# Gate rows for the last expert's result: from a DRAM scratch by transfers instead of from transposes

## The chip, the cores and the metric

The kernel runs on one core of one Trainium2 chip. The metric is device time in microseconds. Of the engines, PE is TensorE (matmuls; PEld its weight loads), DVE is VectorE, ACT is ScalarE, POOL is GpSimd and SP is SyncE, which here only issues transfers. Each engine works through its own instructions in the order of the program. Transfers issued by SP and by ACT are carried out by the same 16 DMA engines.

## The reference, cut to what matters

One layer runs over two streams of 128 tokens with 1024 channels each. A mixer comes first, then a mixture of 32 experts of which each token uses four, then a final norm:

```
x = x + g2 * moe(h)          # g2: one gate value per stream (2) and channel (1024)
moe(h) = sum over e of w_tok[e] * (act_e(h @ w_gu[e] + b_gu[e]) @ w_down[e] + b_down[e])
y = rmsnorm(x) * norm_final
```

The change concerns `g2` where it multiplies the result of the last expert. The values themselves are part of the adaLN modulation and are known long before the experts begin.

## The kernel before

The mixer fills about the first 475 us. After it the experts are worked through one by one, e = 0 to 31, some 27 us each. An expert's weights are six units of 2 MB: units 0 to 3 are quarters of `w_gu`, units 4 and 5 halves of `w_down`. They stream from HBM through eleven places in SBUF; `w31_3` below is unit 3 of expert 31, and where a place is split in two, the halves are called a and b. SP issues each load when PE has read the unit that held its place.

An expert runs so: PE multiplies the gathered tokens by `w_gu` (`e30pgu`, L1229, with the bias at L1235); DVE clamps the one half (`e30gm`, L1255), ACT takes the tanh (`e30tg`, L1256), DVE makes the product (`e30gm`, L1261 and L1262); PE transposes it (`e30pat`, L1299), ACT copies it out (`e30aT`, L1302), and PE multiplies by `w_down` (`e30py`, L1312). Results are added to the tokens two experts at a time: PE scatters a pair's rows with 0/1 matrices `sT` (`e28pc`, L1327), and DVE multiplies by the gate and adds to `xT` (L1177). The last pair is treated apart. The bias rows and expert 30's result are scattered in two batches (`papc`, L1337), one before expert 31's first product and one behind its last.

For expert 31 the gate is applied ahead of the scatter, since that leaves less behind the last matmul: L1528 multiplies `e31py` by a tile `gslot`, in which a channel's gate stands in a column and is repeated down the rows (64 rows of each half of the channels for each stream). `gates_by_slot` (L1494 to L1505) builds it in the SBUF place `spare`, which held `w30_1`. PE transposes the gate columns of `fin`, spread over 128 columns, into a PSUM bank (`pgs`, L1503: 16 transposes of 128x128), and ACT copies the 64 rows that are wanted into `spare` (L1504: four copies). PE's order in the experts is the order in which the code is written; ACT, DVE, SP and POOL are ordered by a scheduler. `fin` itself is filled on POOL at L1018 once the modulation is known.

Each transfer of SP and ACT counts itself done on one of eight counters, DMAHW0 to DMAHW7, which are handed out in turn in the order of the program. A transfer takes a counter only after the transfer that had it before has landed, and the wait for that stands at the issuing engine, ahead of the issue. So each transfer waits for the one eight places earlier, whichever of the two engines issued that one.

Of the kernel before, what the change touches and what calls it, by code (L numbers as in the profile page):

```python
# [9 lines left out]
F32 = mybir.dt.float32  # L10
# [10 lines left out]
P = 128  # L21
D = 1024
# [5 lines left out]
CAP = 64  # L28
# [35 lines left out]
def hybrid_step(ctx, tc, A):  # L64
    nc = tc.nc
    V, S, G, PE = nc.vector, nc.scalar, nc.gpsimd, nc.tensor
# [14 lines left out]
    phase = weights.enter_context(ExitStack())  # L81
    s1 = phase.enter_context(tc.tile_pool(name="s1", bufs=1))
    ps = ctx.enter_context(tc.tile_pool(name="ps", bufs=1, space=PSUM))
    dr = mixer.enter_context(tc.tile_pool(name="dr", bufs=1, space=bass.MemoryType.DRAM))

    def bank(tag, name, bufs):
        return ps.tile([P, 512], F32, name=name, tag=tag, bufs=bufs)
# [22 lines left out]
    def col(name, j, n=1):  # L110
        return prm[:, COL[name] + j:COL[name] + j + n]
# [29 lines left out]
    ident = con.tile([P, P], F32, name="ident")  # L141
# [796 lines left out]
    for h in range(4):  # L938
        sl, k = slice(4 * h, 4 * h + 4), slice(4 * (h % 2), 4 * (h % 2) + 4)
# [77 lines left out]
    fin = con.tile([P, 3, KC], F32, name="fin")  # L1017
    G.tensor_copy(fin[:, 0:2], mod[:, 40:48, :].rearrange("p k s -> p s k"))  # L1018
    G.tensor_copy(fin[:, 2], col("norm_final", 0, 8))

    lgb = mc.tile([P, 2, NE], F32, name="lgb")
    plr = bank("E", "plr", 1)
# [422 lines left out]
    def expert(e):  # L1445
# [16 lines left out]
        if e > 1:  # L1462
            last = down(e - 1)
            if e % 2:
                scatter_pair(e - 1)
            if e == NE - 1:
                gates_by_slot(spare)

                first = [(ys[e - 1][k // 4][own(0, k // 4), k % 4 * P:(k % 4 + 1) * P], sT[e - 1][own(0, k // 4), k // 4]) for k in range(KC)]
                add_two(bias, first, 0, "C", 2)  # L1470

            load_pieces(6 * e + NUNIT)
# [17 lines left out]
    def own(i, h):  # L1490

        return slice(CAP, P) if i ^ h else slice(0, CAP)
# [3 lines left out]
    def gates_by_slot(spare):  # L1496

        for s in range(2):
            t = spare[:, 512 + 512 * s:1024 + 512 * s]
            for h in range(2):  # L1500
                pt = bank("C", f"pgs{s}{h}", 2)
                for k in range(4):
                    PE.transpose(pt[:, k * P:(k + 1) * P], fin[:, s, 4 * h + k:4 * h + k + 1].to_broadcast([P, P]), ident)  # L1503
                S.copy(t[own(1, h)], pt[own(1, h)])  # L1504
            gslot.append(t)  # L1505

    w = last = mores = None
# [116 lines left out]
def build(nc, ins):  # L1624
    A = {k: nc.dram_tensor(f"in_{k}", v.shape, mybir.dt.from_np(v.dtype), kind="ExternalInput").ap()
         for k, v in ins.items()}
    for k, shape in _OUTS.items():
        A[k] = nc.dram_tensor(k, shape, F32, kind="ExternalOutput").ap()
    with tile.TileContext(nc, schedule_with_timeline_sim=True) as tc:  # L1629
        hybrid_step(tc, A)  # L1630
# [15 lines left out]
```

## Time and profile before

| | us |
|---|---|
| runs (median; lowest to highest) | 1434.77; 1432.7 to 1436.01 |
| profiled execution, its own time | 1434.98 |
| profiled execution, span of the trace | 1433.2 |
| PE busy in the span | 1345.4 (94%) |
| ACT busy in the span | 335.0 (23%) |

The span runs from the first to the last instruction; the 1.8 us around it are the same execution's. A "busy" share is an average over the whole span, in which a mixer bound by PE is followed by experts that also live from the weight stream. What an edit near the end is worth is therefore read from the last 80 us alone.

### The profile page before, as it was taken

How to read it: one execution, taken by the hardware profiler on the slowest of the kernel's cores; microseconds unless marked ns; L12 is line 12 of the kernel's file. 1: busy time of each engine (PE TensorE's matmuls, PEld its weight loads, DVE VectorE, ACT ScalarE, POOL GpSimd, SP SyncE). 2: the span in 40 equal slices, each digit the busy share in tenths (PEclk: the TensorE clock that was granted, in tenths of full speed). 3: DMA queues.
4: the chain of work that ended last, by engine and by line, in shares of the span. 5: the costliest groups of instructions: out<-in, count | busy, mean ns of one | idle time of the engine just before them, and what ended most of it. 6: DMA issues, size and time to landing. Idle time of an engine off the chain costs nothing. (4 is left out here: it accounts for less than half of the span.)

```text
span 1433.2 us, 21073 instructions
## 1 busy us (share of the span) xinstructions
PE 1345.4 (94%) x8637; PEld 798.1 (56%) x8637; DVE 591.3 (41%) x1259; ACT 335.0 (23%) x623; POOL 101.8 (7%) x114
## 2 busy tenths in 40 slices
PE   7999999999999999999999899999999999889897
PEld 3988989898999643443444344344344343343343
DVE  4856879998776322132132222213213212222133
ACT  2534656575664110010000000001000000000011
POOL 1112313431002000000000000000000000000000
PEclk8999999999999999999999999999999999999998
DMA  9997566556877899999999999999999999999981
GB/s 359 294 277 190 201 228 233 214 187 221 314 285 264 331 404 424 425 426 423 423 425 426 412 424 423 424 426 424 423 425 426 423 426 424 426 424 425 424 346 37
DMA packets 84717, 506.52 MB, mean 353 GB/s; under 512 B 6850, under 2 KB 35138, under 8 KB 52418
## 3 DMA queue, kind: packets, MB, share of 16 engines
q1 hardware_dynamic: 81666, 497.71, 87.2%
q10 hardware_dynamic: 2880, 6.60, 1.3%
q8 instruction: 98, 1.61, 0.5%
q14 instruction: 73, 0.60, 0.1%
HBM read 498.26 MB, written 5.64 MB: 352 GB/s over the span
## 5 line engine op out<-in xcount | busy, mean ns | idle before, releaser
L303 DVE TENSOR_TENSOR wl<-win,wh 128x1024 fp32r<-128x1024 f32 (+1 forms) x84 | 101.2, 1216 | 35.7 <-ACT wh L302 23.6
L302 ACT CAST wh<-win 128x1024 fp32r<-128x1024 f32 (+1 forms) x84 | 83.9, 1010 | 72.4 <-PE pbc L330 19.2
L193 POOL TENSOR_TENSOR rf<-rf0v,mhalf 128x1 f32<-128x1 f32 x1 | 0.9, 860 | 948.8 <-DVE rf0v L191 948.8
L714 POOL TENSOR_TENSOR m<-m_half,adt 128x512 fp32r<-128x512 f32 x32 | 43.4, 1374 | 87.1 <-PE pss L717 87.1
L330 PE MATMUL pxs<-hT,wh 128*128 128x256 f32 x256 | 37.5, 291 | 0.0
L330 PE MATMUL pz<-hT,wh 128*128 128x256 f32 x256 | 36.7, 288 | 0.0
L330 PE MATMUL pgt<-hT,wh 128*128 128x256 f32 x256 | 36.0, 287 | 0.3 <-ACT wh L302 0.3
L330 PE MATMUL pbc<-hT,wh 128*128 128x256 f32 x256 | 35.6, 287 | 0.0
L330 PEld LDWEIGHTS pxs<-hT,wh 128*128 128x128 f32 x256 | 32.5, 190 | 3.6 <-issue 2.8
L330 PE MATMUL pso<-yhl,wh 128*128 128x256 f32 x256 | 34.1, 284 | 0.0
L330 PEld LDWEIGHTS pgt<-hT,wh 128*128 128x128 f32 x256 | 32.4, 191 | 2.3 <-issue 1.9
L330 PEld LDWEIGHTS pz<-hT,wh 128*128 128x128 f32 x256 | 32.5, 190 | 1.6 <-issue 1.6
L330 PEld LDWEIGHTS pbc<-hT,wh 128*128 128x128 f32 x256 | 32.2, 190 | 1.9 <-issue 1.7
L330 PEld LDWEIGHTS pso<-yhl,wh 128*128 128x128 f32 x256 | 32.1, 192 | 0.0
L330 PE MATMUL pglu<-hT,wh 128*128 128x256 f32 x192 | 26.8, 290 | 0.0
L330 PEld LDWEIGHTS pglu<-hT,wh 128*128 128x128 f32 x192 | 24.8, 197 | 0.7 <-issue 0.7
L303 DVE TENSOR_TENSOR wl<-wso,wh 128x1024 fp32r<-128x1024 f32 x16 | 19.4, 1218 | 7.5 <-ACT wh L302 7.3
L697 ACT ACTIVATE gd<-gm,dtT 128x128 f32<-128x128 f32 x64 | 20.8, 414 | 4.4 <-DVE gm L688 4.3
L698 DVE SCALAR_TENSOR_TENSOR gd<-gm,dtT,gd 128x128 f32<-128x128 f32 x64 | 20.9, 374 | 1.6 <-ACT gd L697 1.2
L302 ACT CAST wh<-wso 128x1024 fp32r<-128x1024 f32 x16 | 16.7, 1046 | 14.3 <-PE pso L330 10.8
L330 PE MATMUL pwo<-mhl,wh 128*128 128x256 f32 x128 | 18.9, 290 | 0.3 <-DVE mhl L1008 0.3
L1229 PE MATMUL e26pgu<-w,xg 128*64 128x512 f32 x64 | 16.1, 656 | 3.2 <-DMA w<-in_w_gu 2.9
(1098 smaller groups left out, 2639.6 us busy)
## 6 DMA issues: line engine op xcount, KB each, us to landing
w<-in_w_gu SPq DMA_DIRECT2D x116, 2048.0 KB, 31.1
w<-in_w_down SPq DMA_DIRECT2D x57, 2048.0 KB, 27.1
win<-in_w_in_pack SPq DMA_DIRECT2D x38, 1024.0 KB, 5.6
ada<-in_w_ada SPq DMA_DIRECT2D x10, 1024.0 KB, 9.0
wso<-in_w_ssd_out SPq DMA_DIRECT2D x8, 1024.0 KB, 5.8
im<-dru SPq DMA_DIRECT2D x16, 312.0 KB, 8.6
wcf<-in_w_conf_out SPq DMA_DIRECT2D x4, 1024.0 KB, 8.6
wo<-in_w_o SPq DMA_DIRECT2D x4, 1024.0 KB, 9.8
```

What stands on the lines that cost most here:

```text
L193: rstd_ins[0] = G.tensor_tensor(r, v, mhalf[:, 0:n], ALU.pow)
L302: S.copy(hi[:, ks, 0:m], w[:, ks])
L303: V.tensor_tensor(lo[:, ks, 0:m], w[:, ks], hi[:, ks, 0:m], ALU.subtract)
L330: last_wo[0] = PE.matmul(out, w[:, k, 0:n], m[:, k, :], start=first and i == 0, stop=last and i == len(order) - 1, skip_group_check=True)
L697: S.activation(gd[s][:, h, :], gm[:, 0, s, :], AF.Copy, scale=dtT[:, 0, s, c0:c0 + 1])
L698: V.scalar_tensor_tensor(gd[s][:, h, :], gm[:, 1, s, :], dtT[:, 0, s, 32 + c0:33 + c0], gd[s][:, h, :], op0=ALU.mult, op1=ALU.add)
L714: G.tensor_tensor(m4[d], m_half[:, d, None, None, :].to_broadcast([P, 2, 4, 64]), ac[d], ALU.mult)
L1229: PE.matmul(banks[i][m * q:m * q + m, 0:wd], xg[:, k, :], w[k][:, c0:c0 + wd], start=(k == 0), stop=False, skip_group_check=True)
```

## The change

The gate rows are no longer made by PE and ACT late in the kernel. Behind the copy that fills `fin`, ACT now issues two transfers that write the two streams' gates, channel after channel, to a DRAM scratch `grow` of 2 x 1024 values (each value is an element of 4 bytes for itself, since a partition of `fin` holds channels 128 apart). In `gates_by_slot` four transfers on ACT's queue read 512 values each and repeat them over 64 rows of `spare`. The 16 transposes and four copies are gone.

```
+    gdr = ctx.enter_context(tc.tile_pool(name="gdr", bufs=1, space=bass.MemoryType.DRAM))
...
     G.tensor_copy(fin[:, 2], col("norm_final", 0, 8))
+    grow = gdr.tile([2, D], F32, name="grow")
+    for s in range(2):
+        S.dma_start(grow[s].rearrange("(k p) -> p k", p=P), fin[:, s])
...
             for h in range(2):
-                pt = bank("C", f"pgs{s}{h}", 2)
-                for k in range(4):
-                    PE.transpose(pt[:, k * P:(k + 1) * P], fin[:, s, 4 * h + k:4 * h + k + 1].to_broadcast([P, P]), ident)
-                S.copy(t[own(1, h)], pt[own(1, h)])
+                S.dma_start(t[own(1, h)], grow[s:s + 1, 512 * h:512 * h + 512].to_broadcast([CAP, 512]))
```

PE's order around expert 30's end, before and then after, loses one piece and nothing else moves (`pst30` are the scatter matrices of experts 30 and 31, `b_dn` the bias rows):

```order
L1283 MATMUL pst30_22459<-ident_126,sg30_22454 128x128 x4
L1503 MATMUL pgs00_22466<-ident_126,fin_5449 128x128 x4
L1503 MATMUL pgs01_22472<-ident_126,fin_5449 128x128 x4
L1503 MATMUL pgs10_22478<-ident_126,fin_5449 128x128 x4
L1503 MATMUL pgs11_22484<-ident_126,fin_5449 128x128 x4
L1337 MATMUL papc00_22490<-spare_22413,b_dn_22414 128x256
```

```order
L1316 MATMUL e30py_22433<-w30_5_21917,e30aT_22430 64x512 x8
L1287 MATMUL pst30_22464<-ident_128,sg30_22459 128x128 x4
L1341 MATMUL papc00_22475<-spare_22418,b_dn_22419 128x256
L1341 MATMUL papc01_22476<-spare_22418,b_dn_22419 128x256
L1341 MATMUL papc00_22475<-spare_22418,b_dn_22419 128x256
```

The 16 transposes between `pst30` and `papc` are gone.

On ACT the place moves. Before, the four copies stood behind expert 30's other work; the rows name what each waits for:

```order
L1256 ACTIVATE e30tg_22375<-e30gm_22374 128x512 [waits DVE_49,Activation_49]
L1302 COPY e30aT_22430<-e30pat_22429 128x512 [waits DVE_49,PE_49]
L1320 COPY y300_22426<-e30py_22428 64x512 [waits PE_49]
L1286 COPY sT30_22464<-pst30_22459 128x512 [waits PE_49]
L1504 COPY spare_22413<-pgs00_22466 64x512 [waits DMAHW4_49,DMAHW3_49,DMAHW7_49,DMAHW0_49,PE_49]
```

After, on ACT, the four transfers stand ahead of the tanh of expert 30:

```order
L1505 DMA spare_22418<-grow_5454 64x512 [waits DMAHW5_49,DMAHW6_49,DMAHW2_49,DMAHW7_49,DMAHW1_49,PE_49]
L1505 DMA spare_22418<-grow_5454 64x512 [waits DMAHW0_49]
L1505 DMA spare_22418<-grow_5454 64x512 [waits DMAHW1_49]
L1505 DMA spare_22418<-grow_5454 64x512 [waits DMAHW2_49]
L1260 ACTIVATE e30tg_22380<-e30gm_22379 128x512 [waits DVE_49,Activation_49]
L1306 COPY e30aT_22435<-e30pat_22434 128x512 [waits DVE_49,PE_49]
L1324 COPY y300_22431<-e30py_22433 64x512 [waits PE_49]
```

They moved ahead of `e30tg`, and they take counters 7, 0, 1 and 2. Who had these counters last stands in SP's order after the change (each load waits for, and then takes, the counter that it names):

```order
L403 DMA w31_0a_21919<-in_w_gu 128x2048 [waits DMAHW6_49,PE_49]
L403 DMA w31_0b_21921<-in_w_gu 128x2048 [waits DMAHW7_49,PE_49]
L403 DMA w31_1_21923<-in_w_gu 128x4096 [waits DMAHW0_49,PE_49]
L403 DMA w31_2_21925<-in_w_gu 128x4096 [waits DMAHW1_49,PE_49]
L403 DMA w31_3_21927<-in_w_gu 128x4096 [waits DMAHW2_49,PE_49]
L403 DMA w31_4_21929<-in_w_down 128x2048 [waits DMAHW3_49,PE_49]
L403 DMA w31_4_21929<-in_w_down 128x2048 [waits DMAHW4_49]
L403 DMA w31_5_22493<-in_w_down 128x2048 [waits DMAHW5_49,PE_49]
L403 DMA w31_5_22493<-in_w_down 128x2048 [waits DMAHW6_49]
```

Counters 7, 0, 1 and 2 were last taken by `w31_0b`, `w31_1`, `w31_2` and `w31_3`, which stand ahead of the four transfers in the program.

In the mixer the two writes of `grow` stand on ACT here:

```order
L698 ACTIVATE gd71_4091<-gm7_4085,dtT_540 128x128 x2
L1023 DMA grow_5454<-fin_5451 128x8x1 [waits DMAHW1_49,Pool_49]
L1023 DMA grow_5454<-fin_5451 128x8x1 [waits DMAHW2_49]
L303 CAST wh77_4409<-win38_4407 128x1024 [waits PE_49]
L895 ACTIVATE gates_1450<-pgt6_4242,bg_278 128x256 [waits PE_49]
```

They come between `gd71` and the cast `wh77`, which followed each other directly before. `wh77` needs the load that counter 1 stands for, so that it waited for that counter itself.

## Rows read from the trace of the kernel before

**Rows 1.** The page: span, and the share of each slice (40 slices)

```profile
span 1433.2 us, 21073 instructions
...
DMA  9997566556877899999999999999999999999981
```

**Rows 2.** Busy time by stretches; columns as the first line says

```profile
core 0: us, PE busy (x) PEld busy (x) DVE busy (x) ACT busy (x) POOL busy (x), PEclk, DMA share, GB/s
1360.00:1370.00 10.00, 6.97 (x32) 2.12 (x32) 0.00 (x0) 0.00 (x0) 0.00 (x0) 1.00 1.01 427
...
1390.00:1400.00 10.00, 9.81 (x50) 3.90 (x48) 2.16 (x8) 0.00 (x0) 0.00 (x0) 1.00 0.27 107
```

**Rows 3.** Timeline of the last experts: start, duration, instruction, idle before it

```profile
1366.96 3.65 PE L1229 MATMUL e30pgu<-w,xg 128*64 128x512 f32 x16 [1.26 <-DMA w<-in_w_gu]
...
1371.66 0.63 ACT L1256 ACTIVATE e30tg<-e30gm 128x512 f32<-128x512 f32 x1 [18.19 <-DVE e30gm L1255]
...
1373.19 0.68 DVE L1261 SCALAR_TENSOR_TENSOR e30gm<-e30tg,e30gm 128x512 f32<-128x512 f32 x1
...
1373.79 1.12 DVE L1177 SCALAR_TENSOR_TENSOR xT<-e28pc,fin,xT 128x128 f32<-128x128 f32 x4
...
1375.06 1.10 PE L1327 MATMUL e28pc<-sT,y 128*128 128x256 f32 x4 [0.43 <-DVE xT L1177]
...
1375.99 0.71 PE L1299 MATMUL e30pat<-ident,e30gm 128*128 128x128 f32 x4
...
1377.38 7.09 PE L1312 MATMUL e30py<-w,e30aT 128*64 128x512 f32 x32 [0.68 <-ACT e30aT L1302]
...
1384.89 1.04 PE L1503 MATMUL pgs<-ident,fin 128*128 128x128 f32 x8
...
1385.12 0.69 DVE L1320 COPY y<-e30py 64x512 f32<-64x512 f32 x1 [6.19 <-ACT y L1320]
1385.70 2.50 ACT L1504 COPY spare<-pgs 64x512 f32<-64x512 f32 x4
...
1389.31 1.13 PE L1337 MATMUL papc<-sT,y 64*128 64x256 f32 x8
...
1390.63 1.94 PE L1229 MATMUL e31pgu<-w_0a,xg 128*64 128x512 f32 x8 [0.19 <-PEq L1368]
```

**Rows 4.** SP's issues of expert 31's weights, same columns

```profile
1351.27 11.13 SPq L402 DMA_DIRECT2D w<-in_w_gu  x3
1366.98 12.56 SPq L402 DMA_DIRECT2D w<-in_w_down  x4
```

**Rows 5.** The last of these three alone, and its time from issue to landing

```profile
1362.07 0.33 SPq L402 DMA_DIRECT2D w<-in_w_gu  x1
...
w<-in_w_gu SPq DMA_DIRECT2D x1, 2048.0 KB, 35.3
```

**Rows 6.** What SP waited for, us in total, times, longest

```profile
SPq L402 <- DMA w<-in_w_gu: 205.7, 51, 5.5
```

**Rows 7.** One source line: ACT's issues of a state, ns min/median/max

```profile
L757 ACTq DMA_DIRECT2D o_state<-sto x8: 338/351/361, 140.7 to 353.5; - x8
```

**Rows 8.** An earlier idle stretch of PE: timeline, and clock by microsecond

```profile
482.77 6.98 PE L1229 MATMUL e0pgu<-w,xg 128*64 128x512 f32 x24 [1.19 <-ACT xg L1211]
...
483.00:484.00 1.00, 1.00 (x4) 0.32 (x4) 0.76 (x5) 0.23 (x2) 0.00 (x0) 0.50 0.58 229
...
486.00:487.00 1.00, 1.00 (x7) 0.31 (x5) 0.17 (x1) 0.00 (x0) 0.00 (x0) 0.97 0.07 25
```

**Rows 9.** The mixer at 350 us: ACT and SP in the timeline

```profile
348.99 1.08 ACT L302 CAST wh<-win 128x1024 fp32r<-128x1024 f32 x1
...
352.90 0.59 ACT L756 COPY sto<-pst 128x512 f32<-128x512 f32 x1 [1.15 <-PE pst L753]
...
376.61 0.38 SPq L94 DMA_DIRECT2D wso<-in_w_ssd_out  x1
```

**Rows 10.** A scratch write of 2048 short rows (L908): time to landing

```profile
DMA to landing us min/median/max: 7.9/7.9/7.9
```

## The prediction

> **What bounds the kernel now.** I read the page first: the slices show the DMA engines busy at nine tenths or more from a third of the span almost to its end, and then nothing [rows 1]. The table by stretches says what that means near the end: until 1370 the DMA share is 1.0 and PE works 7 of 10 us, in 1390 to 1400 the share is down to 0.27 and PE works 9.8 of 10 [rows 2]. So PE waits for weights up to expert 30's last product by `w_gu` (1366.96, which waited 1.26 us for its load), and from there to the end PE and the short chains between its products set the time. The chain through expert 30 is in the timeline: `e30tg` on ACT at 1371.66, `e30pat` at 1375.99, `e30py` at 1377.38 with 7.09 us, `pgs` from 1384.89, and `e31pgu` at 1390.63 [rows 3]. From there to the end of the span there are 42.6 us, which the change leaves as they are. Next I read SP's queue, since the new transfers share its counters: SP issues three units of expert 31 from 1351.27 on, the third at 1362.07, and that one lands 35.3 us later, at 1397.4 [rows 4, 5]. PE reads it after 48 of the 64 parts of `e31pgu`, at 0.22 us a part (32 parts of `e30py` take 7.09) 10.6 us behind 1390.63, at 1401.2; so before the change nobody waits for this landing.
>
> **The change part by part.** The sum is made against the profiled execution, 1434.98 us, which is 0.2 us over the median of the runs shown.
>
> *The 16 transposes and four copies.* PE is free at about 1384.8, when `pgs` starts, and the second batch of `papc` starts at 1389.31. Without `pgs` its inputs decide: DVE's copy of `y` ends at 1385.12 + 0.69 = 1385.8, and the first batch of `papc` (of the second's length, 1.1 us) is through at 1385.9 [rows 3]. So 1389.3 - 1385.9 = 3.4 us go from PE's path. That is the gain, and if nothing else came up it would be the whole result.
>
> *The four reads, and what stands behind them.* ACT has `e30tg` queued directly behind them. The fourth takes counter 2, which `w31_3` holds, and by the kernel's rule it must wait until `w31_3` has landed. That such a wait holds the issuing engine is shown for SP: 51 waits of its loads for earlier loads of `w_gu`, 205.7 us in total [rows 6]; the issue at 1366.98, which takes over the counter of the eighth load before it, comes 0.02 us after PE saw that load landed at 1366.96 [rows 3, 4]. So ACT stands from the end of expert 29's copies until 1397.4, issues the fourth (0.35 us, as its other issues [rows 7]) and reaches `e30tg` at 1397.7 instead of 1371.66: +26.1 us. All of expert 31's loads are issued by 1379.5 [rows 4], and what they waited for lies ahead of the tanh, so the landing doesn't move with the wait. PE has nothing to do meanwhile: `e30pat` needs DVE's product, the product needs the tanh, and every matmul behind stands in order.
>
> The Trainium skill, "DMA: Bandwidth & Descriptors", section "Anatomy of one DMA — SWDGE (gpsimd) path", says that any wait for a semaphore takes place on the issuing sequencer before dispatch, and the DMA engines just consume their queues. By that rule ACT is held too and the sum stands; the trace agrees for SP (205.7 us) and has no wait of ACT of this kind.
>
> *The bytes.* Each read writes 64 x 512 x 4 = 131 kB. The first three are issued while the stream is still running; their 0.39 MB at the 427 GB/s of a full stretch [rows 2] are 0.9 us if all of it stands ahead of `w31_3`, and nothing if none does. I take 0.5, since the stream thins out there. The fourth lands long before L1528 asks for it.
>
> *Behind the tanh.* Before, `e30pat` began 1375.99 - 1372.29 = 3.7 us after the tanh. After the wait, DVE's clamps and its first four additions are already done; what remains is a product (0.68), four additions (1.12) and the last scatter (1.10), 2.9 us in all [rows 3]: -0.8.
>
> *The clock.* PE will have stood for some 25 us. After an idle stretch at 481 to 483 the granted clock was 0.5, the lower level, and at 486 it was back at 0.97; 24 parts of `e0pgu` took 6.98 us there, while `e30py` does 32 in 7.09, so 24 in 5.3: a price of 1.7 us [rows 3, 8]. The bounds are nothing and a doubling of all that follows the wait up to `e30py`'s end (1.10 + 0.71 + 7.09 = 8.9). I take 2.0, near the row, a little more since small matmuls stretch the cold part.
>
> *The two writes of `grow`.* Two issues of 0.35 us on ACT at 349, before casts that start at 348.99. ACT stands idle for 1.15 us at 352.9 [rows 9], which takes it up: 0, or 0.7 if the cover is gone. Their 1024 elements of 4 bytes each are not like anything in the trace; the nearest is a scratch write of 2048 rows, which lands in 7.9 us [rows 10]. Two such one after the other are done 15.8 us later, at 366; the first that needs a counter of theirs is SP's load at 376.61 [rows 9]. So 0 here.
>
> Sum: -3.4 + 26.1 + 0.5 - 0.8 + 2.0 + 0 = +24.4, so 1434.98 + 24.4 = **1459.4 us**. Its own range, with the bounds of clock, bytes and writes cut to what I hold likely, and some 2 us for the landing, is 1455 to 1464.
>
> **The rivals.**
>
> *The gain alone.* If ACT were not held, either since the wait doesn't stand in ACT's order or since the four loads land before it, only the 3.4 us would be left: 1431.6. For it: ACT has 18 us of idle time ahead of `e30tg` [rows 3], and the four loads are issued early. Expert 31 would just bear it: `w31_3` would be wanted at 1401.2 - 3.4 = 1397.8 and lands at 1397.4. Against it: landing minus issue is 35 us, twice that idle time. It decides if the landing were ahead of 1371.
>
> *A shorter wait.* Should the landing that counts be that of the unit before, issued some 5.9 us earlier with the same 35.3 us [rows 4, 5], all terms stay and the wait shrinks: 1453.5. For it: units land close behind each other once the stream thins. Against it: `w31_3` holds the counter by name.
>
> *Slow scatter on top.* If the writes of `grow` took more than the 27 us from 349.5 to 376.61, SP's loads of the mixer would queue behind them, and the stream, full from a third of the span on [rows 1], would carry the delay to the end. The Trainium skill, same page, section "Rules for kernel authors", says that a strided last dimension is lowered to one descriptor per element. By that these are 2048 descriptors of 4 bytes; no row has such, and rows 10 with as many short ones stays under the limit. At twice the price of that row for each write they end at 349.5 + 31.6, 4.5 us late: 1464.
>
> **How the numbers follow.** Forecast 0.82, a shorter wait 0.06, slow scatter or a clock near its upper bound 0.06, the gain alone 0.06 (of which 0.01 falls back to no change). Less than 0.2%, 2.9 us, can't be told from no change. So faster 0.05, same 0.01, slower 0.94. The range of 1453 to 1464.5 holds the forecast's own range and the shorter wait and leaves out the gain and the worst of the clock.
>
> **What would show it.** In the profile after: `e30tg` at about 1398, queued behind a wait of ACT's sequencer for the load of `w_gu`; PE idle for 22 to 25 us ahead of the last `e28pc` and `e30pat`; the clock at 0.5 there; `e30py` longer than 7.09; no `pgs`, and some 2.7 us from the end of `e30py` to `e31pgu` where there were 6.2; no other idle stretch of PE that is new, at 350 above all. The prediction is wrong if `e30tg` stays within 10 us of `e30pgu`'s end, or if the loads that hold the four counters land before it.

## The result and the profile after

The changed kernel took 1457.24 us in the median of four runs (1455.85 to 1462.4), beside 1435.09 of the kernel before (the three runs listed above and a fourth of 1435.4): a ratio of 1.0171, 95% interval 1.0155 to 1.0187. It is slower, as forecast, at 1457.2 against 1459.4. Run again for the experiments it took 1461.08 (five runs, 1457.98 to 1463.31; ratio 1.0185, 1.0164 to 1.0206), so the forecast lies between the two series. The profiled run was the slowest of its four: 1462.4 us, span 1460.6.

The timeline of the changed kernel answers to [rows 3, 4] (start, duration, instruction, idle time before it and what ended it; ACTq and SPq are the issues of ACT and SP):

```profile
1367.53 3.65 PE L1233 MATMUL e30pgu<-w,xg 128*64 128x512 f32 x16 [1.26 <-DMA w<-in_w_gu]
...
1382.35 16.95 ACTq L1505 DMA_DIRECT2D spare<-grow  x4
1399.40 0.63 ACT L1260 ACTIVATE e30tg<-e30gm 128x512 f32<-128x512 f32 x1 [45.35 <-DMA w<-in_w_gu]
...
1401.94 2.04 PE L1331 MATMUL e28pc<-sT,y 128*128 128x256 f32 x4 [26.75 <-DVE xT L1181]
...
1403.78 1.06 PE L1303 MATMUL e30pat<-ident,e30gm 128*128 128x128 f32 x4
...
1405.51 9.76 PE L1316 MATMUL e30py<-w,e30aT 128*64 128x512 f32 x32 [0.68 <-ACT e30aT L1306]
...
1415.79 1.13 PE L1341 MATMUL papc<-spare,b_dn 32*128 32x256 f32 x8
...
1416.85 1.13 PE L1341 MATMUL papc<-sT,y 64*128 64x256 f32 x8
...
1418.17 1.94 PE L1233 MATMUL e31pgu<-w_0a,xg 128*64 128x512 f32 x8 [0.18 <-PEq L1372]
```

ACT's four issues start at 1382.35 and reach to 1399.3, and `e30tg` goes at 1399.40, behind 45.35 us of idle time that a load of `w_gu` ended; before it went at 1371.66. PE stands for 26.75 us ahead of the fourth group of `e28pc`, since its bank waits for DVE's additions, which stand behind the product that needs the tanh. `pgs` is gone: `papc` follows `e30py` at once, and `e31pgu` starts 1418.17 - 1415.27 = 2.90 us after `e30py`'s end, where it was 1390.63 - 1384.47 = 6.16 [rows 3]. But `e28pc`, `e30pat` and `e30py` take 2.04, 1.06 and 9.76 us, where they took 1.10, 0.71 and 7.09.

The source line of the reads shows the issues (duration in ns, then the start of the first and of the last) and the times at which ACT's sequencer stood at a semaphore:

```profile
L1505 ACTq DMA_DIRECT2D spare<-grow x4: 452/452/508, 1382.3 to 1398.8; - x4
L1505 ACTq EVENT_SEMAPHORE  x3: 17/38/38, 1354.2 to 1382.3; - x3
...
DMA to landing us min/median/max: 7.1/7.4/7.7
```

ACT is at the waits from 1354.2 on, passes those of the first read at 1382.3 and issues the fourth at 1398.8; an issue itself takes 0.45 us and a read lands 7.4 us after it. So the transfers are short, and nearly all the time is the wait ahead of them. Which load it is for can be read off for the second read, which takes the counter of `w31_1` (the read in ACT's timeline, then SP's issue of `w31_1` and its landing):

```profile
1387.54 0.45 ACTq L1505 DMA_DIRECT2D spare<-grow  x1
...
L403 SPq DMA_DIRECT2D w<-in_w_gu x1: 328/328/328, 1351.9 to 1351.9; - x1
...
DMA to landing us min/median/max: 35.7/35.7/35.7
```

`w31_1` is issued at 1351.85 and lands 35.7 us later, at 1387.55; the read leaves at 1387.54. The third leaves at 1393.32 and the fourth at 1398.85.

The stretches of that time (columns as in [rows 2]: length, busy time of PE, PEld, DVE, ACT, POOL, then granted clock, DMA share, GB/s):

```profile
1380.00:1390.00 10.00, 0.00 (x0) 0.00 (x0) 0.00 (x0) 0.00 (x0) 0.00 (x0) 0.51 0.87 342
1390.00:1400.00 10.00, 0.00 (x0) 0.00 (x0) 0.00 (x0) 0.60 (x1) 0.00 (x0) 0.50 0.41 160
1400.00:1410.00 10.00, 7.38 (x20) 3.45 (x22) 5.75 (x19) 0.62 (x2) 0.00 (x0) 0.50 0.09 35
```

PE does nothing for 20 us, the granted clock is at its lower level (0.5, so 1.2 GHz), and it stays there until 1410, some 8 us into PE's next work.

### The profile page after: what moved, and what is told of

Same layout as the page of the kernel before. It is cut to its first block, busy times and chain, and to the rows that moved or that the text cites. A ratio compares the mean times of both kernels' runs of the same rounds, so it can differ in the third digit from the quotient of the medians.

```text
span 1460.6 us, 21044 instructions
## 1 busy us (share of the span) xinstructions
PE 1343.8 (92%) x8621; PEld 797.1 (55%) x8621; DVE 589.6 (40%) x1259; ACT 333.0 (23%) x619; POOL 101.4 (7%) x114
## 5 line engine op out<-in xcount | busy, mean ns | idle before, releaser
L1331 PE MATMUL e28pc<-sT,y 128*128 128x256 f32 x16 | 5.2, 464 | 26.7 <-DVE xT L1181 26.7
L303 ACT CAST wh<-wso 128x1024 fp32r<-128x1024 f32 x16 | 16.7, 1047 | 13.4 <-PE pso L331 10.8
```

The source lines that it names most:

```text
L303: S.copy(hi[:, ks, 0:m], w[:, ks])
L1331: ins = PE.matmul(pc[:, i * T:(i + 1) * T], *products[j + i], start=True, stop=True)
```

## The experiments

The theory: ACT is held by the wait of its transfers for counters that the loads of expert 31's weights occupy, and whatever stands behind on ACT waits along. The rivals: the reads themselves cost the time (their bytes, or repeated rows from DRAM), or the 2048 elements of 4 bytes of the two writes do.

**The reads issued by SP.** The changed kernel with one word different.

```
-                S.dma_start(t[own(1, h)], grow[...]...)
+                nc.sync.dma_start(t[own(1, h)], grow[...]...)
```

> The change with the four reads of grow issued on SP's queue, behind the last weight loads, instead of on ACT's. Counter theory (ACT stood in front of the tanh of expert 30 until w31_3 had landed): SP has nothing left to issue but the outputs, so the wait harms nobody and only the gain of the missing transposes is left: 1435.1 - 3.4 = 1431.7 us, e30tg directly behind e30gm, no new idle stretch of PE. Rival 'the reads themselves' (512 kB repeated out of one row of DRAM, beside the weights): the bytes are the same, so 1455 or so stays. Rival 'the scatter' (2048 elements of 4 bytes into DRAM): 1455 stays too.

Measured: 1431.14 us against 1434.76 (ratio 0.9979, 0.9970 to 0.9987). Its timeline:

```profile
1369.73 0.63 ACT L1260 ACTIVATE e30tg<-e30gm 128x512 f32<-128x512 f32 x1 [18.17 <-DVE e30gm L1259]
...
1379.83 17.18 SPq L1505 DMA_DIRECT2D spare<-grow  x4
...
1385.44 1.94 PE L1233 MATMUL e31pgu<-w_0a,xg 128*64 128x512 f32 x8 [0.18 <-PEq L1372]
...
1396.59 1.94 PE L1233 MATMUL e31pgu<-w,xg 128*64 128x512 f32 x8 [0.62 <-DMA w<-in_w_gu]
```

The tanh follows `e30pgu` as it did in the kernel before. SP waits in the reads' place, from 1379.83 to 1397, and has nothing behind them but the output at the very end. `e31pgu` gains what the transposes took. The reads, the writes and the scratch are all still there, so it is neither that costs 22 us. The fourth read leaves SP at 1396.56, and `w31_3`, issued at 1360.16, lands 36.4 us later, at the same moment: the wait is for that load, and the prediction's rival of a shorter wait, for the unit before, falls. What was free before has become a small bound: the last quarter of `w_gu` is now awaited by PE for 0.62 us (1396.59), as the prediction's rival "gain alone" had it at the edge (wanted at 1397.8, landing at 1397.4).

**The reads on ACT, behind the work they held up.**

```
+    last_sT = [None]
...
-        S.copy(sT[e], pst...)
+        last_sT[0] = S.copy(sT[e], pst...)
...
-                S.dma_start(t[own(1, h)], grow[...]...)
+                with tc.issue_after(last_sT[0].ins):
+                    S.dma_start(t[own(1, h)], grow[...]...)
```

`last_sT` is ACT's copy of the scatter matrices, which stands behind `e30py`.

> The change with the four reads left on ACT, but behind the copy of the scatter matrices of experts 30 and 31. Counter theory: ACT is held just as long, to 1399, but what stands behind is the tanh of expert 31, which is not wanted before 1401: 1431.7 us, at most 1433. Rival 'the reads themselves': 1440 or more, since they still run beside the last weights. Rival 'the scatter': 1455.

Measured: 1431.94 us (0.9980, 0.9969 to 0.9990).

```profile
1371.94 0.63 ACT L1260 ACTIVATE e30tg<-e30gm 128x512 f32<-128x512 f32 x1 [18.17 <-DVE e30gm L1259]
...
1385.54 14.24 ACTq L1508 DMA_DIRECT2D spare<-grow  x4
...
1399.34 1.94 PE L1233 MATMUL e31pgu<-w,xg 128*64 128x512 f32 x8 [1.17 <-DMA w<-in_w_gu]
```

The same engine, queue, bytes and waits: from 1385.54 on ACT waits through its four issues again, 14.24 us in all. But nothing that anyone needs stands behind them until the next tanh, and the time is that of the reads on SP. So the loss belongs to the place in ACT's order.

**The two writes alone**, added to the kernel before.

```
+    gdr = ctx.enter_context(tc.tile_pool(name="gdr", ...))
...
+    grow = gdr.tile([2, D], F32, name="grow")
+    for s in range(2):
+        S.dma_start(grow[s].rearrange("(k p) -> p k", p=P), fin[:, s])
```

> The kernel before with the two writes of grow added and nothing else (nobody reads grow). Counter theory: 1435.1, at most +0.7 us; the trace shows two issues of some 0.5 us on ACT at 349 and no idle stretch of PE. Rival 'the scatter': 1450 or more, with SP's loads behind 376 us late.

Measured: 1433.12 us (0.9996, 0.9985 to 1.0007): no cost that can be told. The rival of the slow scatter falls.

**One read, three quarters by transposes.**

```
+                if s == 0 and h == 0:
+                    S.dma_start(t[own(1, h)], grow[...]...)
+                    continue
+                pt = bank("C", f"pgs{s}{h}", 2)
...
```

The lines cut at the end are the transposes and the copy as they were before.

> The change with one read of grow alone, the other three parts of the gate rows by transposes and copies as before. Counter theory: the one read takes counter 7, which w31_0b holds, and that landed at 1382.3 in the trace of the change; so e30tg starts at 1382.8 instead of 1372.2 (+10.6), 0.8 come back behind the tanh, the cold clock costs 4 as in the change, and a quarter of the transposes gone gives 0.9: 1435.1 + 12.9 = 1448. Rival 'the reads themselves' (a cost per read): a quarter of the change's +22, 1440.6.

Measured: 1445.99 us (1.0082, 1.0065 to 1.0098), about half of the loss with a quarter of the bytes.

```profile
1368.63 3.65 PE L1233 MATMUL e30pgu<-w,xg 128*64 128x512 f32 x16 [1.27 <-DMA w<-in_w_gu]
...
1383.44 0.52 ACTq L1506 DMA_DIRECT2D spare<-grow  x1
1384.06 0.63 ACT L1260 ACTIVATE e30tg<-e30gm 128x512 f32<-128x512 f32 x1 [28.91 <-DMA w<-in_w_gu]
...
1390.17 7.09 PE L1316 MATMUL e30py<-w,e30aT 128*64 128x512 f32 x32 [0.68 <-ACT e30aT L1306]
```

The first read's wait alone holds ACT until 1383.44, and `e30tg` goes 15.4 us after the start of `e30pgu`'s last part (1368.63), where it is 4.7 us before and 31.9 with four reads. The hold is set by which load the last of the reads has to wait for. That the time came out 2 us under what was expected is mostly the clock: `e30py` took 7.09 us here, where 9.76 had been reckoned with.

**Four transfers of 8 bytes.** Two tries at the wait with no bytes to speak of, the transposes kept. In the first the transfers went to a tile of their own:

```
+        tiny = sm.tile([1, 16], F32, name="tiny", tag="tiny", bufs=1)
+        for i in range(4):
+            S.dma_start(tiny[:, 4 * i:4 * i + 2], A["c_pack"][0:1, 0, 0:2])
```

> The kernel before, with its transposes and copies, and four transfers of 8 bytes each from an input to a small tile, issued by ScalarE at the very place of the changed kernel's four reads; nobody uses what they bring. Theory (the first of them waits for the counter that `w31_3`'s loads occupy, and ScalarE's `e30tg` stands behind it): `e30tg` leaves at about 1396.8 in place of 1371.66, 25 us later, the cold clock costs 4 more, as measured in the changed kernel, and the 3.3 us that the change takes off the path stay: about 1435 + 25 + 4 - 3 (the part of the transposes' 3.4 us that the later order hides is not known) = 1460 to 1464. Rival (bytes, size or the repeated rows of the reads are what holds ScalarE): 1435.

Measured: 1433.8 us (0.9999, 0.9990 to 1.0009). It tells nothing about the theory: nothing tied the transfers to expert 31, and the scheduler put them where the mixer ends:

```profile
L1500 ACTq DMA_DIRECT2D tiny<-in_c_pack x4: 230/328/502, 485.0 to 486.4; - x4
```

The second writes into the tile that the reads write, which sets the same dependencies and so the same place:

```
+        for s in range(2):
+            for h in range(2):
+                S.dma_start(spare[CAP * (1 - h):CAP * (1 - h) + 1, 512 + 512 * s:514 + 512 * s], A["c_pack"][0:1, 0, 0:2])
```

> The kernel before, its transposes and copies kept, and ahead of `gates_by_slot`'s work four transfers of 8 bytes each, from an input to the first two columns of the four places that the copies fill later. They write the tile that the changed kernel's reads write, so they stand where those stand on ScalarE, ahead of `e30tg`, and their counters come in the same turn. Theory (a wait for a counter that `w31_3`'s loads occupy): `e30tg` leaves at 1396 to 1399 in place of 1371.66, `e28pc` to `e30py` run about 4 us longer at the lower clock, and what the transposes cost TensorE stays: 1435 + 23 to 26 + 4 - 3 (what the hold hides of the 6 us between `e30py` and `e31pgu`, nothing to 3) = 1457 to 1463. Rival (the bytes or the repeated rows of the reads hold ScalarE): 1433 to 1436.

Measured: 1460.39 us beside 1432.95 (1.0191, 1.0171 to 1.0211).

```profile
1365.61 3.65 PE L1229 MATMUL e30pgu<-w,xg 128*64 128x512 f32 x16 [1.26 <-DMA w<-in_w_gu]
...
1380.51 14.77 ACTq L1500 DMA_DIRECT2D spare<-in_c_pack  x4
1395.38 0.63 ACT L1256 ACTIVATE e30tg<-e30gm 128x512 f32<-128x512 f32 x1 [43.25 <-DMA w<-in_w_gu]
...
1401.49 8.81 PE L1312 MATMUL e30py<-w,e30aT 128*64 128x512 f32 x32 [0.67 <-ACT e30aT L1302]
...
1416.46 1.94 PE L1229 MATMUL e31pgu<-w_0a,xg 128*64 128x512 f32 x8 [0.18 <-PEq L1368]
```

32 bytes in four transfers that nobody uses cost as much as the change. This is the plainest proof of the wait. The two sums are made up differently, though: this kernel keeps the transposes, which the change is rid of, and moves almost no bytes. Here `e30tg` goes 29.77 us after the start of `e30pgu`'s last part, and in four profiles with the real reads 31.72 to 31.91 us after it.

**The clock kept up.** The changed kernel with 112 products more, which nobody uses, on PE while ACT is held; and the changed kernel again beside it, since the first comparison was across two series.

```
+            if name == "e28" and j == 6:
+                ft = bank("D", "fillw", 1)
+                for _ in range(112):
+                    PE.matmul(ft, sel3[:, 0:1].to_broadcast([96, P]), b3[:, 0:512], start=True, stop=True, ...)
```

> The changed kernel, with 112 more products of 96 x 128 by 96 x 512 in bfloat16 on TensorE, into a bank that the next user clears, placed ahead of the fourth group of `e28pc`: that is where TensorE stands for 26.75 us while ScalarE is held. They depend on nothing and should end at about 1399, before `e28pc` may run at 1401.9, so they add nothing to the chain. Theory (the part of the loss behind the hold is the lower clock): `e28pc`, `e30pat` and `e30py` take 1.10, 0.71 and 7.09 us again, as [rows 3] have them, in place of 2.04, 1.06 and 9.76: about -4 us, 1453 in place of 1457 in the median, and the hold of ScalarE stays as it was. Rival (the products behind the hold run longer for another reason, such as the transfers landing in the same memory): the durations stay at 2.04, 1.06 and 9.76, and the median at 1457; 1458 or more if the added products end late.

> The changed kernel with the 112 products ahead of the fourth group of `e28pc`, once more. In its profile the stretch from the end of ScalarE's hold to `e31pgu` was 3.9 us shorter than in the changed kernel (14.85 in place of 18.77 us), but the hold ended 1.26 us later and the whole came to 1460 in the median. Theory (the later end is the spread of the loads' landing, which has nothing to do with the products): beside the changed kernel on one chip it is 3 to 4 us faster. Rival (the products, or loading their instructions, delay the loads ahead of the hold, and give back what the clock saves): the two agree within 1 us, and the loads ahead of the hold land about 1 us or more later in this kernel.

> The changed kernel once more, unaltered, beside the next one and on the same chip, since the four runs of each lie 7 and 5 us apart. Both theories: 1456 to 1460.

Measured: 1460.07 us at first (1.0172, 1.0149 to 1.0194), then 1461.56 (1.0196, 1.0173 to 1.0219) beside 1461.08 of the changed kernel. The theory said 3 to 4 us less, and it is no less. Three timelines bear on why. First the one with the products, in their first series:

```profile
1376.25 24.34 PE L1332 MATMUL fillw<-b,sel 96*128 96x512 bf16 x112
...
1400.66 0.63 ACT L1260 ACTIVATE e30tg<-e30gm 128x512 f32<-128x512 f32 x1 [45.38 <-DMA w<-in_w_down]
...
1403.20 1.10 PE L1335 MATMUL e28pc<-sT,y 128*128 128x256 f32 x4 [2.61 <-DVE xT L1181]
...
1405.52 7.09 PE L1316 MATMUL e30py<-w,e30aT 128*64 128x512 f32 x32 [0.68 <-ACT e30aT L1306]
...
1415.51 1.94 PE L1233 MATMUL e31pgu<-w_0a,xg 128*64 128x512 f32 x8 [0.19 <-PEq L1376]
```

The load that the profile names behind the wait of `e30tg` is `w_down` here; the first of its halves was issued at 1368.77 and lands 34.6 us later, at 1403.4, so that the name seems to be a slip of the profile. The theory's mechanism works in this profile: `e28pc` and `e30py` take 1.10 and 7.09 us again, and `e31pgu` 14.85 us after `e30tg` in place of 18.77. Then the same kernel in the second series, with its granted clock:

```profile
1401.10 0.63 ACT L1260 ACTIVATE e30tg<-e30gm 128x512 f32<-128x512 f32 x1 [45.20 <-DMA w<-in_w_gu]
...
1403.63 2.05 PE L1335 MATMUL e28pc<-sT,y 128*128 128x256 f32 x4 [2.41 <-DVE xT L1181]
...
1407.21 7.09 PE L1316 MATMUL e30py<-w,e30aT 128*64 128x512 f32 x32 [0.68 <-ACT e30aT L1306]
...
1417.19 1.94 PE L1233 MATMUL e31pgu<-w_0a,xg 128*64 128x512 f32 x8 [0.18 <-PEq L1376]
```

```profile
1402.00:1404.00 2.00, 0.37 (x1) 0.40 (x2) 2.00 (x7) 0.00 (x0) 0.00 (x0) 0.79 0.18 64
1404.00:1406.00 2.00, 2.00 (x7) 1.54 (x7) 2.00 (x8) 0.00 (x0) 0.00 (x0) 0.50 0.06 24
```

PE had been busy until 1401.2 and stood for 2.4 us only, and yet the clock fell to its lower level (0.79 in the mean of one stretch, 0.50 in the next) and stretched the small matmuls as in the changed kernel, `e28pc` to 2.05. And the changed kernel itself, in the second series:

```profile
1371.17 3.65 PE L1233 MATMUL e30pgu<-w,xg 128*64 128x512 f32 x16 [1.25 <-DMA w<-in_w_gu]
...
1402.99 0.63 ACT L1260 ACTIVATE e30tg<-e30gm 128x512 f32<-128x512 f32 x1 [45.30 <-DMA w<-in_w_gu]
...
1405.53 2.04 PE L1331 MATMUL e28pc<-sT,y 128*128 128x256 f32 x4 [26.70 <-DVE xT L1181]
...
1409.10 7.09 PE L1316 MATMUL e30py<-w,e30aT 128*64 128x512 f32 x32 [0.68 <-ACT e30aT L1306]
...
1419.09 1.94 PE L1233 MATMUL e31pgu<-w_0a,xg 128*64 128x512 f32 x8 [0.18 <-PEq L1372]
```

Without any help `e30py` took 7.09 us, although PE had stood for 26.70 us: `e31pgu` came 16.10 us after `e30tg`, against 18.77 in the first profile and 16.09 in the one above with the products. So the same instructions pay 1.3 us in one run and 4.0 in another, and the products could save only what was lost. That they delay the loads ahead of the hold does not show: in these two profiles `e30pgu`'s last part starts at 1369.38 with them and at 1371.17 without. They also cost something of their own: with them in the program DVE's order in the last stage came out otherwise, and from `e31pgu` to the end it took 43.0 to 43.1 us in place of 42.4. Whether the unprofiled runs of the changed kernel pay 1.3 or 4.0 more often is not known.

## Why the prediction was right

Step by step, from the two profiles of the changed kernel (first and second series) against the one before; the moments are the start of `e30pgu`'s last part, of `e30tg`, the end of `e30py`, the start of `e31pgu`, and the end of the span.

| stretch | before | forecast | first | second |
|---|---|---|---|---|
| up to `e30pgu`'s last part | 1366.96 | 0 | +0.57 | +4.21 |
| to `e30tg` | 4.70 | +26.1 +0.5 | +27.17 | +27.12 |
| to the end of `e30py` | 12.81 | -0.8 +2.0 | +3.06 | +0.39 |
| to `e31pgu` | 6.16 | -3.4 | -3.26 | -3.26 |
| to the end | 42.57 | 0 | -0.14 | -0.16 |
| sum | | +24.4 | +27.40 | +28.30 |

**The wait** came as worked out, on ACT, behind the fourth read, for the load that [rows 5] shows. From the issue of `w31_3` to the fourth read's it is 1398.85 - 1362.63 = 36.2 us, and 36.2 in the second profile, where the forecast had a landing after 35.3 and 0.5 for the bytes. The issue took 0.45 us, not 0.35. PE stood for 26.75 us, a little more than the 22 to 25 that were given as a sign.

**The bytes** were taken too small at 0.5, and how much they cost is not settled. Against the kernel before, the landing that counts came 36.2 - 35.3 = 0.9 us later, and 1.1 with the reads on SP: about the upper bound of 0.9 that the prediction gave. Against the 8-byte transfers, which hold ACT as the reads do, it is more: there the fourth leaves 1395.06 - 1360.72 = 34.3 us after the issue of `w31_3`, so that the reads' bytes would cost 1.9 us. But in that kernel the load landed 1.0 us sooner than in the kernel before, which has no such bytes either; no run shows why, and there is one profile of it. The bound came from dividing 0.39 MB by the full stream's rate, and the stream no longer runs at it where most of the reads fall. The kernel before shows it (columns as in [rows 2]):

```profile
1385.00:1390.00 5.00, 4.52 (x31) 3.11 (x31) 0.69 (x1) 2.99 (x6) 0.00 (x0) 1.00 0.70 290
```

At these 290 GB/s 0.39 MB would be 1.3 us, an estimate that lies between the two readings.

**The clock and the work behind the tanh**, 1.2 us together in the forecast, were 3.1 in one profile and 0.4 in the other. The -0.8 was reckoned with `e28pc` at 1.10 us, which ran at 2.04: from the tanh's end to `e30pat` it is 1403.78 - 1400.03 = 3.75 us, as before. In the first profile with the products, where the clock stayed up, it is 2.85, so that term was right by itself. The clock's own price is the longer durations, 0.94 + 0.35 and in the first profile 2.67 more: 1.3 or 4.0, around the forecast's 2.0 and far from the upper bound of 8.9. That `e30py` would be longer than 7.09 held in the first profile and not in the second.

**The gain** of 3.4 us is there, 3.26, and it is what remains once the wait is out of the way: with the reads on SP the median is 3.6 us lower (3.0 by the ratio), although 0.62 us goes back to PE's wait for `w31_3`.

**The writes of `grow`** cost nothing, as taken, but not because they are light. In the view of DMA queues for 345 to 352 us they are the second line:

```profile
q1 hardware_dynamic: 1044, 1.05, 47.6%
q10 hardware_dynamic: 2080, 0.01, 13.4%
```

2080 packets carry 0.01 MB and take 13.4% of sixteen engines' time in these 7 us. The Trainium skill ("DMA: Bandwidth & Descriptors", "Rules for kernel authors") warned of one descriptor per element, and the count agrees with the 2048 elements. They are over by 352. What follows them is slow: ACT's next transfer, 256 kB of state issued at 354.77, lands after 7.2 us, where none of its kind took more than 4.3 in the kernel before, and SP's load of `wso` issued beside it takes 9.4 us in place of 5.5. From 356 to 358 the DMA share is 1.14 at 26 GB/s. That the writes leave this behind is likely, since the kernel with the writes alone shows it too (7.0 and 9.5 us); by what means is not shown. The mixer takes it up. SP's next transfer that PE's progress releases goes at 378.30 instead of 377.04, but SP was as far behind ahead of the writes, at 344.73 instead of 343.48, and the writes alone do not change the time.

**The lead.** The largest difference between the two profiles is none of the steps. The start of `e30pgu`'s last part lies between 1365.04 and 1371.17 in the eleven profiles of this case, without order: 1365.61, 1366.96 and 1368.55 in the three kernels without the writes of `grow`, the two ends in kernels with them. That is as wide as the spread of one kernel's runs. In the first profile the lead cost little and the clock 4.0, in the second the lead 4.2 and the clock 1.3, and the sums came close to each other, 3 to 4 us above the forecast. Both are profiles of the slowest run of their series (1462.4 and 1463.31 us), so the table accounts for these two runs and not for the medians, which lie 22.2 and 28.1 us above the kernel before. Why these differ is open; the experiments ran on three chips, and whether the chip matters was not tested. So the mechanism was right, but that the first median came within 2.2 us of the forecast is in part luck: the four runs behind it lie up to 6.5 us apart.

## What to carry to other kernels

When work is moved from a compute engine to transfers, look at what that engine has queued behind the issue: a transfer that must wait for a completion counter holds everything behind it, and the counter can belong to a load of another engine's that lands 35 us after its issue. Four transfers of 8 bytes cost as much here as four of 131 kB. Put such an issue on an engine with nothing behind it, or behind the work that the path needs, and the small gain that was the aim appears: both versions that did so are faster than the kernel before, by 0.2%.

## What the runs showed of the hardware

- The place of the issue was worth 26 us: 1457.2 us on ACT ahead of the tanh, 1431.1 on SP, 1431.9 on ACT behind the work. The Trainium skill ("DMA: Bandwidth & Descriptors", "Rules for kernel authors") says that spreading transfers over the engines for bandwidth doesn't help and only saves the time of issuing. The issues here take 0.45 us each; the wait ahead of them is what counted.
- The granted clock fell to 0.5 behind a stand of 2.4 us in one profile, and did not in another of the same kernel behind 2.6 us.
- The 32 products of one column in the last stage (`ssl`) took 5.28 us in the kernel before and 5.56 in the changed one, but 3.93 in the kernels with the reads behind and with the 8-byte transfers in place. The granted clock differs (columns as in [rows 2]). The first line is of the changed kernel, where they start at 1446.52, the second of the 8-byte transfers, where they start at 1444.82:

```profile
1448.50:1450.00 1.50, 1.49 (x7) 1.49 (x8) 0.49 (x1) 0.56 (x1) 0.00 (x0) 0.50 0.00 0
1446.80:1448.80 2.00, 1.95 (x16) 1.86 (x16) 0.50 (x2) 0.55 (x1) 0.00 (x0) 1.00 0.00 0
```

  In the changed kernel the clock fell to 0.50 about 2 us into these products, while PE was at work on them; in the other it stayed at 1.00 until they were through. In the kernel with one read it fell some 3 us in, and they took 4.50 us. It is up to 1.6 us at the end of the path, and it does not go with the change: of the two kernels that carry the reads without harm, one has 3.93 us and the other, with the reads on SP, 5.57.
